# Two of the three split products of a tile put side by side: PEER queries, late up-projection tiles, second FFN

## The chip, the cores and the metric

The kernel runs on one core of one Trainium2 chip. The metric is device time in microseconds (us) of one launch; the kernel before takes 3022.41 us (median of three runs, 3020.68 to 3022.94). The core has TensorE (PE: products; PEld its weight loads), VectorE (DVE), ScalarE (ACT), GpSimd (POOL) and SyncE (SP, which issues most DMAs). Each works through its own instructions in the order in which the program lists them.

## The reference, cut to what matters

Two blocks of two layers work on 256 tokens of width 1024. The first block has a mixer and PEER in each of its layers, the second attention and a gated feed-forward network (FFN) in each. What the change touches:

```python
q = (xt @ wq).reshape(t, PEER_HEADS, D_KEY)        # 16 tiles of 128 query rows
s1 = einsum("thd,hnd->thn", q1, k1); s2 = ...      # scores against 128 + 128 keys
v1, i1 = lax.top_k(s1, TOPK); v2, i2 = ...         # then top 16 of the 16*16 sums
gates = softmax(sv)                                # of 16 of 16384 experts a head
hid = gelu(einsum("td,tkd->tk", xi, u_tab[ei]))    # up-projection
out = einsum("tk,tkd->td", gi * hid, v_tab[ei])    # down-projection
# FFN of the second block:  (silu(x @ Wg) * (x @ Wu)) @ Wo
```

## The kernel before, in words

Activations lie transposed, features on the 128 partitions and tokens (T = 256) along the free axis. Every large fp32 product is made of three: the weights `w` and the input `x` are each split in a high and a low part of type fp32r (wh, wl; hi, lo), and hi·wh, lo·wh and hi·wl are added up in PSUM. `gemm` (L464 to L475) issues these three for each of the kc slices of 128 input features, through `mm` (all at L430); a tile of 1024 input features has kc = 8, so 24 products of 128x256.

Weights come in tiles of 512 KB through `Stream`: SP loads each into one of four `st` buffers; two tiles before it is used, ACT rounds it (CAST `wh`, L381) and DVE subtracts (TENSOR_TENSOR `wl`, L381). There are three `wh`/`wl` buffers, so this split waits until PE is done with the tile three before.

PEER (its layers at about 143 to 960 us and 1104 to 1920 us) first makes the queries: 16 tiles from "wq". After tile b's products, `score(b)` (L1082 to L1094) has ACT copy the PSUM tile to `qt` (L1085) and PE multiply it by the keys into `sc0` and `sc1`; after every fourth tile ACT copies the scores out. On PE, score(b) stands behind the products of tile b+1; the tag `mm` has two PSUM buffers. While this runs, a generator `topk` (L1212 to L1349) puts the search for the best 16 (MAX, MAX_INDEX, MATCH_REPLACE on DVE) between the other work: after each weight tile, `pump` takes pieces from it up to a budget of estimated ns (PUMP0 500, later PUMP 1100 and PUMP2 1400). Then follow 128 "u" tiles (up-projection; PE also makes the gates by one-hot products, `gtok` tokens of them complete) and 128 "v" tiles (down-projection). The reference's picking of 16 experts is done densely: all 16384 hidden values are made and multiplied by gates that are mostly zero. `hid` (L1200 to L1210) finishes a u tile: ACT makes gelu from PSUM, DVE multiplies by the gates where they are complete.

`ffn` (L1845 to L1922) is called with N = 512 columns (first FFN, even layer, 2200 to 2580 us) and with N = 256 (second FFN, odd layer, 2819 to 3013 us). For each of NFF = 22 feature tiles it makes two products (tags mm0, mm1, two buffers each), silu on ACT and a product on DVE, which is split again into fh and fl; then 8 output tiles (out of tag mm0) end in `finish` (L1809, one DVE instruction for each token half).

The order on each engine is set when the program is built: the Python code gives it in outline, and a scheduler with its own estimates of time moves what is free to move.

Of the kernel before, what the change touches and what calls it, by code (L numbers as in the profile page):

```python
# [10 lines left out]
F32R = mybir.dt.float32r  # L11
# [401 lines left out]
class Builder:  # L413
# [50 lines left out]
    def gemm(self, ps, w, kc, rhs, k0=0, first=True, last=True, order=None):  # L464
        hi, lo = w
        order = order or range(kc)
        for n, k in enumerate(order):
            a = hi[:, k * P:(k + 1) * P]
            b = lo[:, k * P:(k + 1) * P]
            rh, rl = rhs(k0 + k)  # L470
            with self.after(self.gends[:1] if n == 0 and len(self.gends) in GP else []):
                self.mm(ps, a, rh, start=first and n == 0)
            self.mm(ps, a, rl)
            self.mm(ps, b, rh, stop=last and n == kc - 1)
        self.gends.append(self.lastmm)  # L475

    def rsq(self, ss, n, pool, tag="rs", bufs=None, ln=False, eps=EPS):
# [569 lines left out]
    def peer(self, l):  # L1047
        nc, tc = self.nc, self.tc
        with tc.tile_pool(name=f"pe{l}", bufs=1) as sp, tc.tile_pool(name=f"pew{l}", bufs=2) as wk, \
# [4 lines left out]
            self.iota8 = self.t(sp, [P, 16, 8], F16, tag="iota8")  # L1054
            self.iota4 = self.t(sp, [P, 4 * P], F16, tag="iota4")
            with tc.tile_pool(name=f"peh{l}", bufs=1) as hp:
                hi = self.t(hp, [P, KD, T], F32R, tag="hi")
                lo = self.t(hp, [P, KD, T], F32R, tag="lo")
                flat = big.rearrange("p j t -> p (j t)")
                front = Carve(flat[:, :4096], 4096)  # L1060
                tail = Carve(flat[:, J0 * T:], (P - J0) * T)
                pk = self.t(tail, [P, 2, 1024], tag="pk", bufs=1)
                for n in range(2):
                    nc.gpsimd.dma_start(pk[:, n], self.I["pk"][l, n])
                self.warm(pp, "g", WP[0], 2)
                ss = self.sumsq((self.t(self.psp, [P, 512], tag="pss", bufs=1) if FD & 1 else self.t(pp, [P, 512], tag="mm"))[:, :T])
                self.warm(pp, "g", WP[1], 2)
                r = self.rsq(ss, T, front, tag="nrm", bufs=1)
                self.norm(self.x, lambda k: self.g(f"norm2_g{l}", k), None, hi, lo, front, r)
                with self.after(self.nins):  # L1070
                    nc.vector.tensor_copy(self.iota8, self.iota[:, :16].unsqueeze(2).to_broadcast([P, 16, 8]))
                    nc.vector.tensor_copy(self.iota4.rearrange("p (i t) -> p i t", t=4),
                                          self.iota.unsqueeze(2).to_broadcast([P, P, 4]))
                nc.gpsimd.dma_start(self.xd[l], self.x)
                self.ohp = Carve(self.x.rearrange("p k t -> p (k t)"), KD * T)
                self.ocp = Carve(self.sreg, 4 * T)
                rhs = lambda k: (hi[:, k, :], lo[:, k, :])
                sc = [self.t(tail, [P, 16, P], tag="sc") for _ in range(2)]
                scp = None
                pend = []  # L1080

                def score(b, ps):  # L1082
                    nonlocal scp
                    qt = self.t(front, [P, T], tag="qt")
                    nc.scalar.copy(qt, ps)  # L1085
                    if b % 4 == 0:
                        scp = [self.t(pp, [P, 4, P], tag=f"sc{t}", bufs=1) for t in range(2)]
                    key = pk[:, b % 2, (b // 2) * P:(b // 2 + 1) * P]
                    for t in range(2):
                        self.mm(scp[t][:, b % 4, :], qt[:, t * P:(t + 1) * P], key, start=True, stop=True)  # L1090
                    if b % 4 == 3:
                        for t in range(2):
                            nc.scalar.copy(sc[t][:, b - 3:b + 1, :], scp[t])
                        self.scored = b + 1  # L1094

                self.J, self.gtok, self.scored = 0, 0, 0
                self.tkdone = False
                self.bg.append(self.topk(l, sc, tail, wk, pp))
                for b in range(16):
                    w = self.stream.get("wq", (l, b), 0, 1024)  # L1100
                    ps = self.t(pp, [P, 512], tag="mm")[:, :T]
                    self.gemm(ps, w, KD, rhs)
                    self.pump(PUMP0)
                    if pend:
                        score(*pend.pop())
                    pend.append((b, ps))
                score(*pend.pop())
                for j in range(P):
                    if j == J0:
                        while not self.tkdone:  # L1110
                            self.pump(1)
                    w = self.stream.get("u", (l, j), 0, 1024)
                    ps = self.t(pp, [P, 512], tag="mm")[:, :T]
                    self.gemm(ps, w, KD, rhs)
                    self.pump(PUMP if j < J0 else PUMP2)
                    if pend:
                        self.hid(*pend.pop(), wk)
                    pend.append((j, ps))
                self.hid(*pend.pop(), wk)
                self.drain()  # L1120
            if self.stop == f"hid{l}":
# [75 lines left out]
        if self.stop == f"peer{l}":  # L1197
            nc.sync.dma_start(self.dump["x"], self.x)

    def hid(self, j, ps, wk):  # L1200
        nc = self.nc
        tk = self.gtok
        dst = self.big[:, j, :]
        if tk:
            tmp = self.t(wk, [P, T], tag="gl")
            self.af(tmp[:, :tk], ps[:, :tk], AF.Gelu_apprx_tanh)
            nc.vector.tensor_mul(dst[:, :tk], dst[:, :tk], tmp[:, :tk])
        if tk < T:
            self.af(dst[:, tk:], ps[:, tk:], AF.Gelu_apprx_tanh)
        self.J = j + 1  # L1210

    def topk(self, l, sc, tl, wk, pp):  # L1212
# [632 lines left out]
    def ffn(self, l, N):  # L1845
        nc, tc = self.nc, self.tc
        with tc.tile_pool(name=f"ff{l}", bufs=1) as sp, tc.tile_pool(name=f"ffw{l}", bufs=2) as wk, \
                tc.tile_pool(name=f"ffp{l}", bufs=2, space=PSUM) as pp:
            fh = self.t(sp, [P, NFF, N], F32R, tag="fh")
            fl = self.t(sp, [P, NFF, N], F32R, tag="fl")  # L1850
            mb = self.t(wk, [P, KD * T], tag="mb", bufs=1)
            nw = Carve(mb, KD * T)
            md = iter(())
# [5 lines left out]
                    next(md, None)  # L1859

            with tc.tile_pool(name=f"ffh{l}", bufs=1) as hp:
                hi = self.t(hp, [P, KD, N], F32R, tag="hi")
                lo = self.t(hp, [P, KD, N], F32R, tag="lo")
                for m in range(N // T - 1, -1, -1):
                    W = (WF0, WF1)[l]
                    if m == 0:
# [7 lines left out]
                    self.modnorm(l, 1, m, hi[:, :, q], lo[:, :, q], nw, r)  # L1874
                rhs = lambda k: (hi[:, k, :], lo[:, k, :])
                for f in range(NFF):
                    pg = [self.t(pp, [P, 512], tag=f"mm{n}")[:, :N] for n in range(2)]
                    sl = self.t(wk, [P, N], tag="sl")
                    if f == 0 and N > T:
                        W = [self.stream.get("fi", (l, f, n), 0, 1024) for n in range(2)]  # L1880
                        for h in range(2):
                            q = slice(h * T, h * T + T)
                            for n in range(2):
                                hrhs = lambda k: (hi[:, k, q], lo[:, k, q])
                                self.gemm(pg[n][:, q], W[n], KD, hrhs, first=h == 0)
                        self.af(sl, pg[0], AF.Silu)
                    else:
                        for n in range(2):
                            w = self.stream.get("fi", (l, f, n), 0, 1024)
                            self.gemm(pg[n], w, KD, rhs)  # L1890
                            side()
                            if n == 0:
                                self.af(sl, pg[0], AF.Silu)
                    nc.vector.tensor_mul(sl, sl, pg[1])
                    nc.scalar.copy(fh[:, f, :], sl)
                    nc.vector.tensor_sub(fl[:, f, :], sl, fh[:, f, :])
# [3 lines left out]
            for b in range(KD):  # L1900
# [1 line left out]
                    self.tables(ARS)  # L1902
                split = b == KD - 1 and N > T
                W = []
                ps = self.t(pp, [P, 512], tag="mm0")[:, :N]
                k0 = 0
                for kc in kcs:
                    W.append(self.stream.get("fo", (l, b), k0 * P, kc * P))
                    if not split:
                        self.gemm(ps, W[-1], kc, lambda k: (fh[:, k, :], fl[:, k, :]), k0=k0, first=k0 == 0,  # L1910
                                  last=k0 + kc == NFF)
                    k0 += kc
                for m in range(N // T - 1, -1, -1):
                    q = slice(N - T - m * T, N - m * T)
                    if split:
                        ps = self.t(pp, [P, 512], tag=f"mm{m}")[:, :N]
                        k0 = 0
                        for w, kc in zip(W, kcs):
                            self.gemm(ps[:, q], w, kc, lambda k: (fh[:, k, q], fl[:, k, q]), k0=k0, first=k0 == 0,
                                      last=k0 + kc == NFF)  # L1920
                            k0 += kc
                    self.finish(l, 1, b, ps[:, q], m, wk)  # L1922

    def odd(self):
# [174 lines left out]
```

## Time and profile before

| | |
|---|---|
| Median of three runs | 3022.41 us |
| Profiled execution | 3020.7 us, its span 3018.9 us |
| PE busy | 2933.6 us (97%), 19072 products |
| PE's mean granted clock | 0.991 of full speed |
| DVE busy | 2250.0 us (75%) |
| ACT busy | 1704.3 us (56%) |
| Down-projection "v" tiles, both layers | about 2 x 360 us, not touched by the change |

Busy shares are averages over the whole span. Stages differ: in the u tiles PE is full and DVE half full, in the query stage both are full. Read a change from the stage in which it stands.

### The profile page before, as it was taken

The numbers are of one execution on the slowest core, as the hardware profiler recorded it, in microseconds if no ns is written. First come the engines' busy times: TensorE is split into PE (matmuls) and PEld (weight loads), VectorE is DVE, ScalarE is ACT, GpSimd is POOL, SyncE is SP. The second block draws the span as 40 slices with busy tenths as digits, with TensorE's granted clock in tenths as the row PEclk, the third lists the DMA queues.
The fourth block names the chain that finished last, engine by engine and source line by source line (L and its number), as shares of the span: only waits on it lengthen the run. The fifth ranks groups of instructions, "written<-read, shape, count | busy, mean of one in ns | idle before, by whom it ended". The sixth has DMA issues, their size and how long they took to land.

```text
span 3018.9 us, 50427 instructions
## 1 busy us (share of the span) xinstructions
PE 2933.6 (97%) x19072; PEld 2595.6 (86%) x19072; DVE 2250.0 (75%) x4353; ACT 1704.3 (56%) x2931; POOL 215.4 (7%) x259
## 2 busy tenths in 40 slices
PE   8999999999999899999999999998999999999999
PEld 7899999977888889999997788875688878976899
DVE  8799699699556969879969855677577773478654
ACT  7546799544444655589944444467532222377443
POOL 4200000000001710000000000100120001100100
PEclk8999999999999999999999999999999999999999
DMA  5456555588665445655568766511146553331454
GB/s 158 146 161 182 170 159 156 173 291 258 192 194 171 142 136 173 182 163 158 156 213 282 236 192 194 155 59 42 53 130 186 181 185 107 105 105 56 151 183 149
DMA packets 133603, 489.35 MB, mean 162 GB/s; under 512 B 15024, under 2 KB 15280, under 8 KB 132208
## 3 DMA queue, kind: packets, MB, share of 16 engines
q1 hardware_dynamic: 130608, 472.65, 51.0%
q0 software_dynamic: 2608, 13.44, 1.3%
q8 instruction: 150, 2.46, 0.3%
q14 instruction: 93, 0.76, 0.1%
q10 hardware_dynamic: 144, 0.05, 0.0%
HBM read 480.83 MB, written 5.24 MB: 161 GB/s over the span
## 4 chain that ended last, share of the span: by engine, by line
PE 57%; DVE 3%; ACT 2%; issue 1%; DMA 0%; DVEq 0%; ACTq 0%; SPq 0%
PE mm L430 39%; PE g L430 7%; PE sc L430 6%; PE s L430 3%; PE o L430 1%; PE pt L1752 1%; PE pss L430 1%; ACT wh L381 0%; DVE lo L637 0%; PE ss L430 0%; PE pss L1365 0%; ACT grsy L498 0%; DVE wl L381 0%; DVE hi L637 0%; DVE mb L637 0%
## 5 line engine op out<-in xcount | busy, mean ns | idle before, releaser
L381 ACT CAST wh<-st 128x1024 fp32r<-128x1024 f32 (+1 forms) x797 | 831.6, 1045 | 921.5 <-PE mm L430 506.7
L381 DVE TENSOR_TENSOR wl<-st,wh 128x1024 fp32r<-128x1024 f32 (+1 forms) x797 | 977.1, 1227 | 447.8 <-ACT wh L381 440.2
L430 PE MATMUL mm<-hi,wh 128*128 128x256 f32 (+1 forms) x3552 | 1083.0, 306 | 11.8 <-DVE hi L637 7.2
L430 PE MATMUL mm<-hi,wl 128*128 128x256 f32 (+1 forms) x3552 | 1066.0, 301 | 8.0 <-DVE wl L381 7.8
L430 PE MATMUL mm<-lo,wh 128*128 128x256 f32 (+1 forms) x3552 | 1065.3, 300 | 3.0 <-DVE lo L637 2.9
L430 PEld LDWEIGHTS mm<-hi,wh 128*128 128x128 f32 x3552 | 680.4, 192 | 44.6 <-issue 7.6
L430 PEld LDWEIGHTS mm<-hi,wl 128*128 128x128 f32 x3552 | 682.5, 192 | 30.2 <-DVE wl L381 9.2
L430 PEld LDWEIGHTS mm<-lo,wh 128*128 128x128 f32 x3552 | 683.3, 192 | 26.8 <-DVE lo L637 5.9
L430 PE MATMUL sc<-wl,wwh 128*128 128x512 f32 x496 | 195.1, 393 | 0.0
L430 PE MATMUL g<-wl,wwh 128*128 128x512 f32 x496 | 193.1, 389 | 0.0
L430 PE MATMUL g<-wh,wwl 128*128 128x512 f32 x496 | 193.1, 389 | 0.0
L430 PE MATMUL sc<-wh,wwl 128*128 128x512 f32 x496 | 193.1, 389 | 0.0
L430 PE MATMUL sc<-wh,wwh 128*128 128x512 f32 x496 | 192.3, 389 | 0.0
L430 PE MATMUL g<-wh,wwh 128*128 128x512 f32 x496 | 192.3, 389 | 0.0
L1154 ACT CAST wwh<-big 128x512 fp32r<-128x512 f32 x124 | 77.1, 624 | 148.4 <-PE g L430 148.3
L1329 ACT COPY sreg<-x 128x512 f16<-128x512 f16 x256 | 158.3, 661 | 0.0
L1397 DVE SCALAR_TENSOR_TENSOR sreg<-mb,silc,sreg 128x512 f32<-128x512 f32 x168 | 116.9, 745 | 10.8 <-DMA mb<-in_mod 10.5
L1397 DVE SCALAR_TENSOR_TENSOR sreg<-tl,silc,sreg 128x512 f32<-128x512 f32 x168 | 119.8, 747 | 4.7 <-DMA tl<-in_mod 4.6
L430 PE MATMUL mm<-fl,wh 128*128 128x256 f32 (+1 forms) x374 | 122.4, 327 | 0.0
L430 PE MATMUL mm<-fh,wh 128*128 128x256 f32 (+1 forms) x374 | 122.4, 327 | 0.0
L430 PE MATMUL mm<-fh,wl 128*128 128x256 f32 (+1 forms) x374 | 122.3, 327 | 0.0
L1155 DVE TENSOR_TENSOR wwl<-big,wwh 128x512 fp32r<-128x512 f32 x124 | 85.4, 690 | 48.1 <-ACT wwh L1154 48.0
(550 smaller groups left out, 4518.2 us busy)
## 6 DMA issues: line engine op xcount, KB each, us to landing
st<-in_u SPq DMA_DIRECT2D x256, 512.0 KB, 3.7
st<-in_v SPq DMA_DIRECT2D x256, 512.0 KB, 3.7
st<-in_fi SPq DMA_DIRECT2D x88, 512.0 KB, 3.4
st<-in_w SPq DMA_DIRECT2D x58, 512.0 KB, 3.7
tl<-in_mod SPq DMA_DIRECT2D x48, 512.0 KB, 4.9
mb<-in_mod SPq DMA_DIRECT2D x48, 512.0 KB, 4.3
st<-in_wq SPq DMA_DIRECT2D x32, 512.0 KB, 4.3
st<-in_fo SPq DMA_DIRECT2D x32, 512.0 KB, 3.6
```

The lines of the kernel that those rows point to most:

```text
L381: self.last = [b.nc.scalar.copy(hi, t).ins, b.nc.vector.tensor_sub(lo, t, hi).ins]
L430: self.lastmm = self.nc.tensor.matmul(out, lhsT=a, rhs=b, start=start, stop=stop, skip_group_check=True).ins
L1154: nc.scalar.copy(wh, big[:, j:j + 2, :])
L1155: nc.vector.tensor_sub(wl, big[:, j:j + 2, :], wh)
L1329: nc.scalar.copy(oc[m], o[:, m].rearrange("p i t -> p t i"))
L1397: nc.vector.scalar_tensor_tensor(a, w[:, k % 2], s, a, op0=OP.mult, op1=OP.add)
L1752: nc.tensor.transpose(pt[:, b, :], A[qt][:, b * P:(b + 1) * P], self.ident)
```

## The change

A function `gemm2` makes the three products as two instructions. High and low part of the input lie side by side in one buffer `hl` of [128, kc, 2, 256]; per slice, one product of 512 columns gives wh·hi in the left half of a PSUM bank and wh·lo in the right half, and one of 256 columns adds wl·hi to the left half. The columns streamed are the same, 768 for each slice; one product and one weight load fewer are issued. The two halves have to be added afterwards. The change uses `gemm2` in three places:

- the 16 query tiles of both PEER layers (2 x 16 x 8 = 256 slices); in `score` ACT copies the right half and DVE adds the left
- the u tiles whose gates are complete when they are made: 19 in each layer (2 x 19 x 8 = 304 slices); in `hid` ACT copies, DVE adds, ACT then makes gelu from SBUF, DVE multiplies
- the second FFN: 44 input tiles (352 slices) with copy and add, and 8 output tiles of 22 slices (176), where `finish` runs once for each half

Together 1088 slices. No DMA is added or taken away.

```diff
+    def gemm2(self, ps, w, kc, hl, k0=0, first=True, last=True):
+        hi, lo = w
+        for n in range(kc):
+            self.mm(ps, hi[:, n * P:(n + 1) * P], hl[:, k0 + n], start=first and n == 0)
+            self.mm(ps[:, :T], lo[:, n * P:(n + 1) * P], hl[:, k0 + n, 0], stop=last and n == kc - 1)
+        self.gends.append(self.lastmm)
...
                 def score(b, ps):
                     qt = self.t(front, [P, T], tag="qt")
-                    nc.scalar.copy(qt, ps)
+                    nc.scalar.copy(qt, ps[:, T:])
+                    nc.vector.tensor_add(qt, qt, ps[:, :T])
...
-                    self.gemm(ps, w, KD, rhs)
+                    self.gemm2(ps, w, KD, hl)
                     self.pump(PUMP0)
...
+                    pair = self.gtok == T
+                    if pair:
+                        self.gemm2(ps, w, KD, hl)
+                    else:
+                        self.gemm(ps[:, :T], w, KD, rhs)
...
+        if pair:
+            tmp = self.t(wk, [P, T], tag="gl")
+            nc.scalar.copy(tmp, ps[:, T:])
+            nc.vector.tensor_add(tmp, tmp, ps[:, :T])
+            self.af(tmp, tmp, AF.Gelu_apprx_tanh)
+            nc.vector.tensor_mul(dst, dst, tmp)
...
+                                self.gemm2(pg[n], w, KD, hl)
+                                sm = self.t(wk, [P, T], tag=f"sm{n}")
+                                nc.scalar.copy(sm, pg[n][:, T:])
+                                nc.vector.tensor_add(sm, sm, pg[n][:, :T])
+                                pg[n] = sm
...
+                    if N == T:
+                        self.finish(l, 1, b, ps[:, T:], m, wk)
                     self.finish(l, 1, b, ps[:, q], m, wk)
```

DVE, query stage of the first PEER layer, before, from the split of tile 7 (`wl36`) on. `big` is the buffer in which the top-k search works, `mm` a PSUM tile:

```order
L381 TENSOR_TENSOR wl36_1892<-st36_1755,wh36_1891 128x1024
L1228 MAX big_185_1656<-big_185_1656 128x8 x8
L1229 MAX_INDEX big_185_1656<-big_185_1656 128x8
L1231 MATCH_REPLACE big_185_1656<-big_185_1656 128x128
L1229 MAX_INDEX big_185_1656<-big_185_1656 128x8 x4
L1231 MATCH_REPLACE big_185_1656<-big_185_1656 128x128
L1229 MAX_INDEX big_185_1656<-big_185_1656 128x8 x3
L381 TENSOR_TENSOR wl37_1933<-st37_1791,wh37_1932 128x1024
L1232 MAX big_185_1656<-big_185_1656 128x8 x2
L381 TENSOR_TENSOR wl38_1972<-st38_1825,wh38_1971 128x1024
```

The same place now; `mm_220` and `mm_222` are the query tiles 4 and 5:

```order
L381 TENSOR_TENSOR wl36_1855<-st36_1746,wh36_1854 128x1024
L1093 TENSOR_TENSOR big_185_1656<-big_185_1656,mm_220_1831 128x256
L1246 MAX big_185_1656<-big_185_1656 128x8 x8
L1247 MAX_INDEX big_185_1656<-big_185_1656 128x8
L1249 MATCH_REPLACE big_185_1656<-big_185_1656 128x128
L1247 MAX_INDEX big_185_1656<-big_185_1656 128x8 x4
L1249 MATCH_REPLACE big_185_1656<-big_185_1656 128x128
L1247 MAX_INDEX big_185_1656<-big_185_1656 128x8
L381 TENSOR_TENSOR wl37_1889<-st37_1775,wh37_1888 128x1024
L1247 MAX_INDEX big_185_1656<-big_185_1656 128x8 x2
L1093 TENSOR_TENSOR big_185_1656<-big_185_1656,mm_222_1860 128x256
L1250 MAX big_185_1656<-big_185_1656 128x8 x2
```

The top-k pieces stand where they stood but for two of MAX_INDEX; an add of 128x256 now stands behind each `wl`, for tile 5 with a piece of the search between the two.

ACT in the u tiles with complete gates, before, from the rounding of the weights of u tile 118 on (`gl` is the gelu's result):

```order
L381 CAST wh163_7675<-st163_7543 128x1024
L498 ACTIVATE gl_829_7706<-mm_826_7647 128x256
L381 CAST wh164_7709<-st164_7577 128x1024
L498 ACTIVATE gl_831_7740<-mm_828_7681 128x256
L381 CAST wh165_7743<-st165_7611 128x1024
L498 ACTIVATE gl_833_7774<-mm_830_7715 128x256
```

And now:

```order
L381 CAST wh163_7518<-st163_7410 128x1024
L1218 COPY gl_828_7541<-mm_825_7496 128x256
L505 ACTIVATE gl_826_7513<-gl_826_7513 128x256
L505 ACTIVATE gl_828_7541<-gl_828_7541 128x256
L381 CAST wh164_7546<-st164_7438 128x1024
L1218 COPY gl_830_7569<-mm_827_7524 128x256
L381 CAST wh165_7574<-st165_7466 128x1024
L1218 COPY gl_832_7597<-mm_829_7552 128x256
L505 ACTIVATE gl_830_7569<-gl_830_7569 128x256
```

Before, each rounding of weights is followed by one gelu. Now a copy takes the gelu's place, and the gelus come in twos, so that every second rounding stands behind two of them. On DVE the multiplications come in twos in the same way, between the adds.

## Rows read from the trace of the kernel before

**Rows 1.** The page: busy us (share of the span), instructions.

```profile
PE 2933.6 (97%) x19072; PEld 2595.6 (86%) x19072; DVE 2250.0 (75%) x4353; ACT 1704.3 (56%) x2931; POOL 215.4 (7%) x259
```

**Rows 2.** The page: chain of work that ended last, shares by engine.

```profile
PE 57%; DVE 3%; ACT 2%; issue 1%; DMA 0%; DVEq 0%; ACTq 0%; SPq 0%
```

**Rows 3.** Windows: us; busy (instructions) of PE, PEld, DVE, ACT, POOL; PEclk, DMA share, GB/s.

```profile
160.00:200.00 40.00, 40.00 (x339) 40.00 (x339) 37.91 (x180) 18.75 (x30) 0.00 (x0) 1.00 0.53 151
200.00:240.00 40.00, 40.00 (x334) 39.84 (x333) 40.00 (x192) 23.11 (x33) 0.00 (x0) 1.00 0.59 181
240.00:280.00 40.00, 39.89 (x333) 39.69 (x332) 39.09 (x117) 22.63 (x35) 0.00 (x0) 1.00 0.60 175
560.00:600.00 40.00, 40.00 (x332) 39.82 (x331) 21.52 (x29) 18.44 (x28) 0.00 (x0) 1.00 0.61 184
2840.00:2880.00 40.00, 40.00 (x335) 40.00 (x335) 22.29 (x28) 18.80 (x28) 0.00 (x0) 1.00 0.56 185
1960.00:2160.00 200.00, 190.06 (x757) 131.75 (x756) 144.84 (x358) 137.42 (x309) 3.11 (x6) 1.00 0.14 43
```

**Rows 4.** Timeline of PE, second FFN: start us, duration us, instruction.

```profile
2896.94 0.28 PE L430 MATMUL mm<-lo,wh 128*128 128x256 f32 x1
...
2899.82 0.28 PE L430 MATMUL mm<-lo,wh 128*128 128x256 f32 x1
```

**Rows 5.** Timeline of PE, products of 512 columns.

```profile
859.83 0.39 PE L430 MATMUL g<-wh,wwh 128*128 128x512 f32 x1
...
861.87 0.39 PE L430 MATMUL sc<-wh,wwl 128*128 128x512 f32 x1
```

**Rows 6.** Timeline of PE, query stage: first score, and two later ones.

```profile
151.55 0.71 PE L430 MATMUL sc<-big 128*128 128x128 f32 x4 [1.05 <-ACT big L1085]
...
158.29 0.61 PE L430 MATMUL sc<-big 128*128 128x128 f32 x4
...
161.61 0.61 PE L430 MATMUL sc<-big 128*128 128x128 f32 x4
```

**Rows 7.** Timeline of DVE, query stage: weight splits and first row of three groups.

```profile
151.26 2.44 DVE L381 TENSOR_TENSOR wl<-st,wh 128x1024 fp32r<-128x1024 f32 x2 [1.96 <-ACT wh L381]
...
163.91 1.64 DVE L1228 MAX8 big<-big 128x8 f32<-128x128 f32 x8
...
177.81 1.63 DVE L1228 MAX8 big<-big 128x8 f32<-128x128 f32 x8
...
181.45 1.21 DVE L381 TENSOR_TENSOR wl<-st,wh 128x1024 fp32r<-128x1024 f32 x1
...
182.57 0.09 DVE L1229 MATCH_VALUE_LOAD big<-big 128x8 f32 x1
...
191.44 1.24 DVE L1228 MAX8 big<-big 128x8 f32<-128x128 f32 x6
```

**Rows 8.** Lines L854 (DVE add) and L1085 (ACT copy): durations ns min/median/max.

```profile
L854 DVE TENSOR_TENSOR x<-x,mm x8: 414/421/422, 121.1 to 1094.2; 128x256 f32<-128x256 f32 x8
...
L1085 ACT COPY big<-mm x32: 361/366/375, 151.1 to 1159.8; 128x256 f32<-128x256 f32 x32
```

**Rows 9.** Timeline of ACT and DVE, a late u tile.

```profile
555.67 1.05 ACT L381 CAST wh<-st 128x1024 fp32r<-128x1024 f32 x1 [1.55 <-PE mm L430]
...
556.62 0.38 ACT L498 ACTIVATE gl<-mm 128x256 f32<-128x256 f32 x1
...
556.75 1.22 DVE L381 TENSOR_TENSOR wl<-st,wh 128x1024 fp32r<-128x1024 f32 x1 [1.32 <-ACT wh L381]
...
557.89 0.42 DVE L1207 TENSOR_TENSOR big<-big,gl 128x256 f32<-128x256 f32 x1
```

**Rows 10.** Timeline of DVE and SP: the end.

```profile
3013.37 0.48 DVE L1809 SCALAR_TENSOR_TENSOR x<-mm,mt,x 128x256 f32<-128x256 f32 x1 [6.28 <-PE mm L430]
...
3013.88 0.35 SPq L2071 DMA_DIRECT2D out<-x  x1
```

More of the change, by code (lines that the diff above doesn't have):

```diff
@@ L1056, in peer @@
             with tc.tile_pool(name=f"peh{l}", bufs=1) as hp:
-                hi = self.t(hp, [P, KD, T], F32R, tag="hi")
-                lo = self.t(hp, [P, KD, T], F32R, tag="lo")
+                hl = self.t(hp, [P, KD, 2, T], F32R, tag="hl")
+                hi, lo = hl[:, :, 0], hl[:, :, 1]
                 flat = big.rearrange("p j t -> p (j t)")
@@ L1100, in peer @@
                     w = self.stream.get("wq", (l, b), 0, 1024)
-                    ps = self.t(pp, [P, 512], tag="mm")[:, :T]
-                    self.gemm(ps, w, KD, rhs)
+                    ps = self.t(pp, [P, 512], tag="mm")
+                    self.gemm2(ps, w, KD, hl)
                     self.pump(PUMP0)
@@ L1112, in peer @@
                     w = self.stream.get("u", (l, j), 0, 1024)
-                    ps = self.t(pp, [P, 512], tag="mm")[:, :T]
-                    self.gemm(ps, w, KD, rhs)
+                    ps = self.t(pp, [P, 512], tag="mm")
+                    pair = self.gtok == T
[3 more added lines that the diff above has]
+                        self.gemm(ps[:, :T], w, KD, rhs)
                     self.pump(PUMP if j < J0 else PUMP2)
@@ L1117, in peer @@
                         self.hid(*pend.pop(), wk)
-                    pend.append((j, ps))
+                    pend.append((j, ps, pair))
                 self.hid(*pend.pop(), wk)
@@ L1198, in peer, with hid @@
             nc.sync.dma_start(self.dump["x"], self.x)
-    def hid(self, j, ps, wk):
+    def hid(self, j, ps, pair, wk):
         nc = self.nc
@@ L1203, in hid @@
         dst = self.big[:, j, :]
-        if tk:
+        if pair:
[4 more added lines that the diff above has]
+            nc.vector.tensor_mul(dst, dst, tmp)
+        elif tk:
             tmp = self.t(wk, [P, T], tag="gl")
@@ L1208, in hid @@
         if tk < T:
-            self.af(dst[:, tk:], ps[:, tk:], AF.Gelu_apprx_tanh)
+            self.af(dst[:, tk:], ps[:, tk:T], AF.Gelu_apprx_tanh)
         self.J = j + 1
@@ L1848, in ffn @@
                 tc.tile_pool(name=f"ffp{l}", bufs=2, space=PSUM) as pp:
-            fh = self.t(sp, [P, NFF, N], F32R, tag="fh")
-            fl = self.t(sp, [P, NFF, N], F32R, tag="fl")
+            if N > T:
+                fh = self.t(sp, [P, NFF, N], F32R, tag="fh")
+                fl = self.t(sp, [P, NFF, N], F32R, tag="fl")
+            else:
+                fhl = self.t(sp, [P, NFF, 2, T], F32R, tag="fhl")
+                fh, fl = fhl[:, :, 0], fhl[:, :, 1]
             mb = self.t(wk, [P, KD * T], tag="mb", bufs=1)
@@ L1861, in ffn @@
             with tc.tile_pool(name=f"ffh{l}", bufs=1) as hp:
-                hi = self.t(hp, [P, KD, N], F32R, tag="hi")
-                lo = self.t(hp, [P, KD, N], F32R, tag="lo")
+                if N > T:
+                    hi = self.t(hp, [P, KD, N], F32R, tag="hi")
+                    lo = self.t(hp, [P, KD, N], F32R, tag="lo")
+                else:
+                    hl = self.t(hp, [P, KD, 2, T], F32R, tag="hl")
+                    hi, lo = hl[:, :, 0], hl[:, :, 1]
                 for m in range(N // T - 1, -1, -1):
@@ L1876, in ffn @@
                 for f in range(NFF):
-                    pg = [self.t(pp, [P, 512], tag=f"mm{n}")[:, :N] for n in range(2)]
+                    pg = [self.t(pp, [P, 512], tag=f"mm{n}") for n in range(2)]
                     sl = self.t(wk, [P, N], tag="sl")
@@ L1889, in ffn @@
                             w = self.stream.get("fi", (l, f, n), 0, 1024)
-                            self.gemm(pg[n], w, KD, rhs)
+                            if N > T:
+                                self.gemm(pg[n], w, KD, rhs)
+                            else:
+                                self.gemm2(pg[n], w, KD, hl)
[3 more added lines that the diff above has]
+                                pg[n] = sm
                             side()
@@ L1904, in ffn @@
                 W = []
-                ps = self.t(pp, [P, 512], tag="mm0")[:, :N]
+                ps = self.t(pp, [P, 512], tag="mm0")
                 k0 = 0
@@ L1908, in ffn @@
                     W.append(self.stream.get("fo", (l, b), k0 * P, kc * P))
-                    if not split:
+                    if N == T:
+                        self.gemm2(ps, W[-1], kc, fhl, k0=k0, first=k0 == 0, last=k0 + kc == NFF)
+                    elif not split:
                         self.gemm(ps, W[-1], kc, lambda k: (fh[:, k, :], fl[:, k, :]), k0=k0, first=k0 == 0,
@@ L1921, in ffn @@
                             k0 += kc
+                    if N == T:
+                        self.finish(l, 1, b, ps[:, T:], m, wk)
                     self.finish(l, 1, b, ps[:, q], m, wk)
```

## The prediction

> **What bounds the kernel now.** I read the page first: PE is busy for 97% of the span [rows 1], and the chain of work that ended last runs over PE for 57% of the span and over every other engine for 3% or less [rows 2]. So a PE instruction less is time less, wherever PE has no other reason to wait. Then the windows, stage by stage [rows 3]. In the late u tiles (560 to 600 us) and in the second FFN (2840 to 2880) PE is busy for 40.00 of 40 us, DVE for 21.52 and 22.29, ACT for under 19: room for work on DVE. In the query stage and just behind it (160 to 280) it is otherwise: PE 40.00, 40.00 and 39.89, and DVE 37.91, 40.00 and 39.09. There two engines are full at once, and what is put on DVE there has no gap to go into. Most of the first window's 2.09 us of DVE idle is no reserve either: the top-k search begins only at 163.91 [rows 7]. The change takes time from PE in three stages and gives DVE work in the same three, one of them this one.
>
> **What one pair saves.** Products of 256 columns in the second FFN start 24 apart in 2.88 us, 120.0 ns each [rows 4]; products of 512 columns start nine apart in 2.04 us, 226.7 ns each [rows 5]. Twice the columns cost 106.7 ns more, so 13.3 ns belong to the instruction. Three products of 256 take 360.0 ns, one of 512 and one of 256 take 346.7: 13.3 ns saved a slice, 0.107 us a tile of eight slices, 14.5 us over 1088 slices if nothing else happens. The 24 products of a tile go from 2.88 to 2.77 us.
>
> The Trainium skill, "TensorE: Matmul & The Clock Gate", section "Back-to-back issue gap", gives an isolated gap of columns by 2.4 GHz plus about 2.5 ns. For these fp32r products the trace disagrees, 120.0 and 226.7 ns where that rule has 109 and 216. By the rule a slice would save 2.5 ns, all slices 2.7 us; since the fixed part is measured here, the sum goes by the rows.
>
> **Second FFN: -6.6.** 528 slices by 13.3 ns are -7.0 us. The 44 copies (0.37 us on ACT) and 44 adds (0.42 us on DVE) [rows 8] come to 14 of each in 40 us: 5.2 us on ACT beside 18.80, 5.9 on DVE beside 22.29 [rows 3]. Tags mm0 and mm1 have two buffers each, so the copy and add of a tile have until three tiles later, over 8 us; this work lies beside PE. If that cover were gone, each tile would wait about 0.8 us (copy and add in series), 35 us in all; with half of both engines free I see no reason for it. At the end it does show: the last output tile has two `finish` instructions where there was one of 0.48 us, between PE's last product and the output DMA [rows 10]; since one starts before the other's recorded end, +0.4.
>
> **Late u tiles: -2.4.** 304 slices save 4.0 us if nothing waits. In the trace ACT rounds the next weights at 555.67, makes gelu at 556.62, DVE splits at 556.75 (behind the rounding) and multiplies at 557.89 [rows 9]; the last product of the tile in question starts at 555.47, 0.20 us before that rounding. PE could use the PSUM buffer again when the gelu was done, at 557.00. Now the buffer is free when the add is done, which on DVE stands behind the split, where the multiplication stood: 557.89 + 0.42 = 558.31, 2.84 us after that product's start. PE wants the buffer 0.12 + 2.77 = 2.89 us after it. That is a tie. But ACT's order now has two gelus in a row before every second rounding, and the second of them waits for the add: about 558.3 + 0.38, 558.7 with its signal, where the next rounding could start at about 558.55. So every second tile can be late by up to 0.2 us, which would eat both tiles' 0.21. Bounds: -4.0 (no wait) and +1.7 (a wait of 0.15 in each of the 38 tiles, 5.7 - 4.0). I take a wait behind every fourth tile or so, -1.2 a layer.
>
> **Query stage: +14.0.** PE's tile takes 3.32 us here (161.61 - 158.29 [rows 6]: 2.88 of products, 0.44 of score), four tiles 13.28. DVE's period for four tiles, search and splits, is (191.44 - 163.91)/2 = 13.77 us [rows 7]. So DVE was already 0.49 us a group slower than PE, which the splits' lead of two tiles absorbed. Now four adds join each period. One lasts 0.42 us [rows 8], but DVE's instructions start before the one ahead has ended in the record (a split of 1.21 us has its follower 1.12 after its start [rows 7]), so 0.33 to 0.42; I take 0.38. DVE's period becomes 13.77 + 1.52 = 15.29, PE's own work 13.28 - 0.43 = 12.85. And the lead no longer helps: score(b) waits for add(b) itself, and that stands on DVE behind the split of tile b+3 and, as the order shows, for tile 5 behind a piece of search as well (177.81 to 181.45 is such a piece, 3.6 us [rows 7]). PE's next tile but one waits for the same add through the two `mm` buffers. What queues behind it on DVE is the next split, so PE's wait comes back to DVE as nothing gained. PE takes DVE's pace: 15.29 - 13.28 = 2.0 us a group, three groups between tile 4 and the end of the queries, +6.0 a layer; the saving of PE's pairs in them is gone.
>
> Ahead of the groups the first score waits too. It starts at 151.55, released by ACT's copy [rows 6]; DVE's split of tile 3 starts at 151.26 [rows 7], and its add can follow only at 152.38, ending at 152.80: +1.3. Three tiles between save 0.3. Together +7.0 a layer, +14.0 for both. Following the order instruction by instruction with these durations gives the same within half a microsecond, with waits of about 2 us at scores 5, 9 and 13. PE does not win it back: behind the queries it is full again [rows 3], and everything of the search is late by the same amount. Bounds: -1.5 a layer (every add hidden, the pairs' saving of 14 tiles kept, the first two tiles being bound by their inputs) and +8.6 (1.3, adds of 0.42, and half a microsecond more for each of the three long pieces of search).
>
> **Even attention stage: 0.** The diff does not touch it, but the scheduler now lists ACT's and DVE's instructions there in another order. PE idles 9.94 us of the 200 between 1960 and 2160 [rows 3]. What a new order does to that can't be read from here: bounds -5 and +5, half of that idle time gone or added; I take 0, the present order being as good a guess as any.
>
> **Sum.** 14.0 - 2.4 - 6.6 = +5.0. The profiled execution took 3020.7 us, so 3025.7; the median of the runs shown is 1.7 above that execution, so 3027.4.
>
> **The rivals.**
> *The adds are hidden.* The search gives way, scores don't wait, and PE keeps all its savings: 2 x -1.5, -4.0, -6.6 = -13.6, 3008.8. For it: DVE is busy for only 75% [rows 1], and ACT, which could hold up the copy, has half its time free. Against it: 40.00 of 40 on DVE just where the adds go, and fixed places in its order. 15%.
> *Half is won back.* Score's waits are shorter than the period says, because DVE's idle time of about 3 us in 160 to 280 and the lead of the splits behind the queries take up part of them: +3.5 a layer in place of +7.0, so -2.0, 3020.4. 25%.
> *A wait in the even stage.* The new order there adds 5 us to PE's idle 9.94: +10.0, 3032.4. It decides as soon as some operand of the attention comes later than before; nothing in the trace speaks for or against. 15%.
> *No gain from pairing.* Products of 512 and 256 columns in turn, each with its own weights, are not in this trace; if the pair takes 360 ns as before, the FFN gives +0.4 and the u tiles nothing, +14.4, 3036.8. Against it: both lengths have the same 13.3 ns. This is also about where the page's rule would end. 5%.
>
> **How the numbers follow.** My forecast has 40%: 3027.4, by itself 3023 to 3032. The range of 8 in 10 reaches down towards the hidden adds and up to the unpaired case: 3012 to 3036. About 0.2%, 6 us, is what can be told from no change. Faster than 3016.4 is the first rival and a little of the second, 19%; slower than 3028.4 is about two fifths of the forecast, the even stage, the unpaired case and the rest, 39%; between, 42%.
>
> **What would show it.** In the changed profile: PE idle before `sc` of 1 to 2.5 us, released by DVE's add in `score`, four or more times a layer; the first u tile about 7 us later in the first layer and 13 in the second; PE busy below 37 of 40 in 160 to 200. Pairs starting 347 ns apart, tiles of 2.77 us in the second FFN, and that FFN 6 to 7 us shorter. In the late u tiles waits of PE of under 0.25 us. I am wrong if PE stays at 40.00 in 160 to 200, if the pair takes 360 ns, or if the stages between 1950 and 2820 us change their length by more than 3 us.

## The result: 3043.0 us, slower by 0.7%

| | before | after |
|---|---|---|
| Median | 3022.47 us | 3043.02 us |
| Ratio, 95% interval | | 1.0068 (1.0055 to 1.0081) |
| Profiled execution, its span | 3020.7, 3018.9 us | 3042.9, 3040.8 us |
| PE products | 19072 | 17984 |

The sign was forecast, the size was not: +5 us forecast, +20.5 us measured, outside the range. 19072 - 17984 = 1088 products are gone, as the change says, and the chain of work that ended last now runs over PE for 87% and over DVE for 8% of the span. In the changed profile's page (busy times of the engines, then the shares of the chain) [rows 1, 2]:

```profile
PE 2931.3 (96%) x17984; PEld 2537.9 (83%) x17984; DVE 2292.1 (75%) x4475; ACT 1728.6 (57%) x3013; POOL 215.9 (7%) x259
...
PE 87%; DVE 8%; ACT 3%; issue 1%; DMA 0%; DVEq 0%; ACTq 0%; SPq 0%
```

PE's busy time is only 2.3 us less although over a thousand products are gone, in part because the granted clock was at its lower level for 70.1 us of the span instead of 59.0; and its idle time went from 85.3 us to 109.5.

**Where the time went.** Both programs split the same 797 weight tiles in the same order on DVE, so the start of a split is a landmark that both traces have (they are counted from 0). How much later each starts after the change (us), from DVE's rows at L381:

| landmark | later by |
|---|---|
| weight tile 30, start of the first query stage | -0.03 |
| 154, first paired u tile of layer 0 | +10.72 |
| 300, near the end of layer 0's "v" tiles | +15.02 |
| 330, second query stage | +14.99 |
| 450, before the paired u tiles of layer 1 | +24.27 |
| 600, near the end of layer 1's "v" tiles | +26.95 |
| 640, first FFN | +26.84 |
| 734, second FFN, first tiles | +28.27 |
| last product | +21.39 |
| output DMA | +21.91 |

So the two query stages cost 10.7 and 9.3 us, the late u tiles 4.3 and 2.7, the stages between (the attention of the second block and the first FFN) 1.3 together; the second FFN gained 6.9, and its end gave back 0.5.

**The query stages.** First two of the windows of [rows 3], then PE's waits for scores, in the timeline of PE of the changed kernel:

```profile
160.00:200.00 40.00, 36.21 (x211) 31.29 (x211) 35.42 (x157) 16.33 (x27) 0.00 (x0) 0.96 0.43 134
200.00:240.00 40.00, 38.34 (x304) 37.15 (x303) 39.15 (x192) 19.31 (x29) 0.00 (x0) 1.00 0.51 158
```

```profile
152.84 0.71 PE L430 MATMUL sc<-big 128*128 128x128 f32 x4 [2.26 <-DVE big L1093]
...
172.66 0.71 PE L430 MATMUL sc<-big 128*128 128x128 f32 x4 [1.78 <-DVE big L1093]
...
189.22 0.71 PE L430 MATMUL sc<-big 128*128 128x128 f32 x4 [1.62 <-DVE big L1093]
...
204.57 0.71 PE L430 MATMUL sc<-big 128*128 128x128 f32 x4 [1.54 <-DVE big L1093]
```

Scores 0, 5, 9 and 13 wait, each released by DVE's add at L1093. From the start of the last product to the score these places lost 2.42, 1.94, 1.78 and 1.70 us against a product's normal spacing, scores 7, 11 and 15 another 0.9 together; of the first, 1.21 was there before [rows 6]. That is 7.5 us a layer. Then the clock: windows of 5 us behind the first two of these waits, and one around the third.

```profile
155.00:160.00 5.00, 5.00 (x27) 4.39 (x26) 1.06 (x1) 1.32 (x2) 0.00 (x0) 0.80 0.44 140
...
175.00:180.00 5.00, 5.00 (x26) 4.36 (x25) 3.84 (x20) 1.32 (x2) 0.00 (x0) 0.75 0.36 105
...
185.00:190.00 5.00, 3.38 (x22) 2.77 (x21) 5.00 (x26) 1.97 (x4) 0.00 (x0) 1.00 0.36 102
```

The granted clock stands behind POOL's count: 0.80 and 0.75 over five microseconds in which PE was busy throughout (1.00 around the third wait). In each of the two some five pairs took 641 ns each, 427 and 214, where a pair otherwise takes 347: PE ran at its lower level, 1.2 instead of 2.4 GHz. Each such stretch costs about 1.5 us; there are two in the first layer and one in the second, which is just the difference between 10.7 and 9.3. Waits 7.5, clock 3.0, pairs -1.5 make 9.0 of the 10.7; the last 1.7 (the same in both layers) lies in gaps of 0.1 us or less around the scores and was not followed further.

**The late u tiles.** DVE's timeline at the first paired tiles of layer 0, then PE's at the same place:

```profile
564.66 1.22 DVE L381 TENSOR_TENSOR wl<-st,wh 128x1024 fp32r<-128x1024 f32 x1
565.79 0.75 DVE L1219 TENSOR_TENSOR gl<-gl,mm 128x256 f32<-128x256 f32 x2
566.69 0.76 DVE L1221 TENSOR_TENSOR big<-big,gl 128x256 f32<-128x256 f32 x2
571.94 1.23 DVE L381 TENSOR_TENSOR wl<-st,wh 128x1024 fp32r<-128x1024 f32 x1 [4.49 <-ACT wh L381]
```

```profile
563.13 0.28 PE L430 MATMUL mm<-hl,wl 128*128 128x256 f32 x1
566.35 0.54 PE L430 MATMUL mm<-hl,wh 128*128 128x512 f32 x1 [2.94 <-DVE gl L1219]
```

Two adds in a row (x2): those of the first and of the second paired tile. Both stand on DVE behind a split which can't begin before PE is through with the second of them, at 563.13. So PE has no free PSUM buffer for the third tile, and stands for 2.94 us until the add; the prediction's sign for this stage was waits of under 0.25 us. It stands there in both layers (3.10 us lost each time), and in layer 0 a stretch at a clock of 0.53 follows (566.4 to 570). In the tiles behind, small waits of 0.04 to 0.11 us, up to 0.23 together behind every second tile, come to 1.0 to 1.1 us in 41 us, against 1.55 that the pairs save there.

**The second FFN** does what was worked out. Ten pairs in PE's timeline, and the end on DVE and SP [rows 4, 10]:

```profile
2899.62 0.39 PE L430 MATMUL mm<-hl,wh 128*128 128x512 f32 x1
2899.85 0.28 PE L430 MATMUL mm<-hl,wl 128*128 128x256 f32 x1
...
2903.08 0.39 PE L430 MATMUL mm<-hl,wh 128*128 128x512 f32 x1
```

```profile
3034.76 1.00 DVE L1827 SCALAR_TENSOR_TENSOR x<-mm,mt,x 128x256 f32<-128x256 f32 x2 [5.80 <-PE mm L430]
...
3035.79 0.35 SPq L2108 DMA_DIRECT2D out<-x  x1
```

3.46 us for ten pairs is 346 ns, so the fixed cost of 13.3 ns an instruction holds. The Trainium skill, "TensorE: Matmul & The Clock Gate", section "Back-to-back issue gap", would have this pair at about 325 ns (512 and 256 columns by 2.4 GHz, 2.5 ns each, an estimate from that page's formula for an isolated product); for these products the trace disagrees.

### The profile page after: what moved, and what is told of

Read it like the earlier page. It is cut to its first block, busy times and chain, and to the rows that moved or that the text cites. A ratio compares the mean times of both kernels' runs of the same rounds, so it can differ in the third digit from the quotient of the medians.

```text
span 3040.8 us, 48474 instructions
## 1 busy us (share of the span) xinstructions
PE 2931.3 (96%) x17984; PEld 2537.9 (83%) x17984; DVE 2292.1 (75%) x4475; ACT 1728.6 (57%) x3013; POOL 215.9 (7%) x259
## 4 chain that ended last, share of the span: by engine, by line
PE 87%; DVE 8%; ACT 3%; issue 1%; DMA 0%; DVEq 0%; ACTq 0%; SPq 0%
PE mm L430 54%; PE g L430 13%; PE sc L430 12%; PE s L430 4%; DVE wl L381 2%; PE o L430 1%; DVE cacc L903 1%; PE pss L430 1%; PE pt L1770 1%; ACT wh L381 1%; PE pss L1383 1%; PE ss L430 0%; ACT grsy L505 0%; DVE lo L644 0%; DVE hi L644 0%
## 5 line engine op out<-in xcount | busy, mean ns | idle before, releaser
L381 ACT CAST wh<-st 128x1024 fp32r<-128x1024 f32 (+1 forms) x797 | 831.8, 1045 | 892.4 <-PE mm L430 427.2
L381 DVE TENSOR_TENSOR wl<-st,wh 128x1024 fp32r<-128x1024 f32 (+1 forms) x797 | 980.1, 1231 | 434.6 <-ACT wh L381 429.1
L430 PE MATMUL mm<-hl,wh 128*128 128x256 f32 (+1 forms) x4400 | 978.4, 311 | 14.5 <-DVE gl L1219 5.9
L430 PEld LDWEIGHTS mm<-hl,wh 128*128 128x128 f32 x4400 | 716.9, 192 | 58.8 <-issue 8.1
L430 PE MATMUL mm<-hl,wl 128*128 128x256 f32 x2656 | 751.7, 283 | 0.5 <-DVE wl L381 0.5
L430 PEld LDWEIGHTS mm<-hl,wl 128*128 128x128 f32 x2656 | 510.2, 192 | 1.1 <-DVE wl L381 0.8
L430 PE MATMUL mm<-hi,wh 128*128 128x512 f32 (+1 forms) x896 | 318.2, 358 | 9.0 <-DVE hi L644 5.9
L430 PE MATMUL mm<-hi,wl 128*128 128x512 f32 (+1 forms) x896 | 313.7, 351 | 6.1 <-DVE wl L381 6.1
L430 PE MATMUL mm<-lo,wh 128*128 128x512 f32 (+1 forms) x896 | 312.3, 350 | 1.6 <-DVE lo L644 1.5
L430 PEld LDWEIGHTS mm<-hi,wh 128*128 128x128 f32 x896 | 171.3, 193 | 40.6 <-issue 6.1
L430 PEld LDWEIGHTS mm<-hi,wl 128*128 128x128 f32 x896 | 172.2, 192 | 29.2 <-DVE wl L381 7.6
L430 PEld LDWEIGHTS mm<-lo,wh 128*128 128x128 f32 x896 | 172.1, 192 | 24.1 <-DVE lo L644 3.6
```

Of the source, the lines that this page charges most:

```text
L381: self.last = [b.nc.scalar.copy(hi, t).ins, b.nc.vector.tensor_sub(lo, t, hi).ins]
L430: self.lastmm = self.nc.tensor.matmul(out, lhsT=a, rhs=b, start=start, stop=stop, skip_group_check=True).ins
```

## The experiments

All medians are beside runs of the kernel before on the same chip (3022.5 to 3023.1 us). Ratios are to it, with the 95% interval. "Later by" is the shift of splits as in the table above; where a stage is spoken of, it is from the trace, since the attention stages of the second block differ by up to 5 us each between these profiles, in order and in clock, with no edit in them. Small shifts are not to be read either: in the kernel with the FFN alone, which leaves PEER as it was, the second query stage starts 1.7 us later and ends 0.7 later.

**One stage at a time.** Where a stage is not paired, its products go back to

```diff
-                    self.gemm2(ps, w, KD, hl)
+                    self.gemm(ps[:, :T], w, KD, rhs)
```

and its copy and add go with it. The FFN alone:

> The second FFN alone is paired; queries and u tiles are as before. Theory (the loss comes from DVE's adds in the query stage and the late u tiles, each stage by itself): the FFN keeps its gain, -5 to -6 us, so 3017; the splits of weight tiles 0 to 720 come within 1 us of their times before. Rival (the loss comes from the scheduler's new order of the stages that were not edited, or from pairs as such): not faster than 3022.

Measured 3016.61 us, 0.9978 (0.9968 to 0.9987), faster by 5.9. The two PEER layers end 0.1 and 0.5 us later than before. As the theory had it for the time; only the stages between the PEER layers and the second FFN, 7.1 us longer in this profile (0.5 to 7.6 later), missed the "within 1 us".

The query tiles alone:

> The query tiles alone are paired. Theory: the waits of PE for the adds, +7.6 us a layer, less 1.5 for the pairs, and one or two stretches at the lower granted clock of 1.5 us each behind them: +9 to +11 a layer, 3042. Rival (the loss needs the late u tiles as well, since it is the late search that meets them): +7 a layer or less, 3036 or less.

Measured 3042.43 us, 1.0063 (1.0046 to 1.0080). Later by 11.2 us behind the first query stage and 20.0 behind the second, with the same waits:

```profile
153.32 1.23 PE L430 MATMUL sc<-big 128*128 128x128 f32 x4 [2.25 <-DVE big L1093]
173.13 0.71 PE L430 MATMUL sc<-big 128*128 128x128 f32 x4 [1.78 <-DVE big L1093]
189.69 0.71 PE L430 MATMUL sc<-big 128*128 128x128 f32 x4 [1.56 <-DVE big L1093]
```

The loss of the query stage is its own; it needs no other stage.

The late u tiles alone:

> The late u tiles alone are paired. Theory: one wait of about 3 us a layer at the third paired tile, where both adds stand behind a split that can't start before the second paired tile is done, sometimes 1.5 for the lower clock behind it, and no gain later since ACT's gelus in twos eat it: +2.5 to +4.5 a layer, 3029. Rival (the wait was made by the late search of the paired queries): -1 to -2 a layer, 3020.

Measured 3032.49 us, 1.0033 (1.0020 to 1.0046). Later by 4.3 us behind layer 0 and 6.8 behind layer 1, so 4.3 and 2.5 a layer; another 4.5 us of this profile's difference lie in the stages up to the second FFN. PE's wait is there though the search is on time (in this and some later kernels the add stands at L1218):

```profile
555.59 0.47 PE L430 MATMUL mm<-hl,wh 128*128 128x512 f32 x1 [2.94 <-DVE gl L1218]
```

**Without the add.** In the query stage, paired:

```diff
-                    nc.scalar.copy(qt, ps[:, T:])
-                    nc.vector.tensor_add(qt, qt, ps[:, :T])
+                    nc.scalar.copy(qt, ps[:, :T])
```

> The query tiles alone are paired, and the add is left out: ACT copies the left half, so the part lo*wh is missing from the queries. Theory (the add on DVE is the whole loss): -1.5 us a layer and no wait above half a microsecond but the first score's, 3019.5. Rival (pairs of 512 and 256 columns, or the fuller PSUM tile, cost something there by themselves): 3025 or more.

Measured 3023.58 us, 1.0001 (0.9991 to 1.0011), which is no difference. In the trace the query stages are without loss: earlier by 0.3 us behind the first and 1.2 behind the second, though they began 0.7 and 0.8 later; no wait but the first score's, and PE full where it was at 36.21:

```profile
160.00:200.00 40.00, 40.00 (x253) 35.90 (x252) 37.88 (x178) 19.11 (x32) 0.00 (x0) 1.00 0.51 154
```

So the add on DVE is the whole loss there, not the pair. Counted from their own starts the two stages took 1.0 and 2.0 us less, together the 3 expected, as far as such shifts can be read; what the stages between took back and 4 us in the attention stages covered it in that profile.

**A third PSUM buffer for the u tiles.** In PEER, with the FFN paired and the queries not:

```diff
-                    ps = self.t(pp, [P, 512], tag="mm")
+                    ps = self.t(pp, [P, 512], tag="mm", bufs=3)
```

> Second FFN and late u tiles paired, queries as before, and three PSUM buffers instead of two for the tag mm in PEER. Theory (in the u tiles PE waits for a free PSUM buffer, which the add on DVE releases a tile late): the 3 us wait at the third paired tile and the loss of the steady tiles go, each layer gains up to 2 us; with the FFN's -5.9 the time is 3013. Rival (PE is held there by something else, the splits behind two gelus for one): u tiles stay at +2.5 to +4.3 a layer, 3023.

Measured 3012.95 us, 0.9961 (0.9948 to 0.9974), 10 us faster than before. The long wait has become a short one, before the fourth paired tile instead of the third, and layer 0 gains 1.6 us from its first paired tile on and layer 1 1.8, of 2.0 possible. First PE, then DVE at the same place:

```profile
554.40 0.47 PE L430 MATMUL mm<-hl,wh 128*128 128x512 f32 x1 [0.17 <-DVE gl L1218]
```

```profile
552.70 1.22 DVE L381 TENSOR_TENSOR wl<-st,wh 128x1024 fp32r<-128x1024 f32 x1
553.84 0.75 DVE L1218 TENSOR_TENSOR gl<-gl,mm 128x256 f32<-128x256 f32 x2
```

Both adds still stand behind one split, as in the change. So at this place it was the buffer and not another order that took the wait away.

**Scores two tiles behind.** Query tiles alone paired, adds on DVE, three buffers, and

```diff
-                    if pend:
-                        score(*pend.pop())
+                    if len(pend) > 1:
+                        score(*pend.pop(0))
```

> Query tiles alone paired, adds on DVE as in the change, but score(b) stands two tiles behind instead of one, with three PSUM buffers. Theory (DVE's work per four tiles, 15.3 us, exceeds PE's and sets the pace): most of the loss stays, +4 to +7 us a layer without the first score's wait, 3033. Rival (only the place of the add matters, one tile more of slack hides it): -1 us a layer, 3020.

Measured 3020.18 us, 0.9988 (0.9979 to 0.9998). My theory fell: no wait of note but the first score's, 1.1 us earlier behind the first query stage. With the adds on DVE, PE is full:

```profile
160.00:200.00 40.00, 40.00 (x256) 35.99 (x255) 36.67 (x158) 19.06 (x30) 0.00 (x0) 1.00 0.51 157
```

DVE's work of four tiles is not 15.3 us here. Between the first rows of two groups of the search lie 13.1 and 13.2 us (180.75, 193.82, 207.06), with four splits and three or four adds among them, but less of the search: 6 MATCH_REPLACE instead of 8, 13 MAX instead of 16. The rest of the search stands in the u tiles.

**The add on GpSimd.** FFN and queries paired, ACT copies both halves:

```diff
-                    nc.scalar.copy(qt, ps[:, T:])
-                    nc.vector.tensor_add(qt, qt, ps[:, :T])
+                    qh = self.t(front, [P, 2 * T], tag="qh")
+                    nc.scalar.copy(qh, ps)
+                    nc.gpsimd.tensor_add(qt, qh[:, :T], qh[:, T:])
```

> Second FFN and query tiles paired, u tiles as before; in score ACT copies both halves (512 columns) to SBUF and GpSimd adds them there, nothing is added on DVE. Theory (DVE is the full engine, ACT and GpSimd have room): the query stage gains its 1.5 us a layer or is within 1 us of before, 3014 with the FFN's -5.9. Rival (any second step between products and score costs, or GpSimd slows DVE down): +3 us a layer or more, 3022 or more.

Measured 3015.45 us, 0.9978 (0.9968 to 0.9988). The query stage is within 1 us of before (later by 0.6 behind the first, by 0.0 behind the second; counted from their starts, 0.5 and 1.3 shorter), as the theory's second case has it; the pairs' 1.5 us a layer don't show in full. GpSimd takes 0.73 to 1.81 us for an add that takes DVE 0.42 [rows 8]; two of the 32:

```profile
157.46 1.28 POOL L1094 TENSOR_TENSOR big<-big 128x256 f32<-128x256 f32 x1 [1.67 <-ACT big L1093]
161.09 1.30 POOL L1094 TENSOR_TENSOR big<-big 128x256 f32<-128x256 f32 x1 [2.35 <-ACT big L1093]
```

All three stages paired, this add and three buffers:

> All three stages paired, with the add of the query stage on GpSimd as in the kernel with GpSimd's add, and three PSUM buffers for mm. Theory: the gains add up, -5.9 for the FFN, -1 a layer for the queries, -1.5 a layer for the u tiles: 3011. Rival (the stages hinder each other): 3017 or more, not better than the FFN alone.

Measured 3013.80 us, 0.9967 (0.9953 to 0.9981): better than before, but no better than without paired queries.

**What the third buffer does.** Query tiles alone paired, score one tile behind as in the change, three buffers:

> Query tiles alone paired, adds on DVE, score(b) one tile behind as in the change, three PSUM buffers for mm. It parts the two things that the kernel with late scores changed together. Theory (score itself waits for the add, so the place of the score is what matters): waits before sc stay, +3 to +9 us a layer, 3030 or more. Rival (the missing thing was a PSUM buffer for the products behind): no waits but the first, -1 a layer, 3020.5.

Measured 3019.84 us, 0.9992 (0.9983 to 1.0002). My theory fell again, and the rival had the time right: no wait of note but the first score's (1.90 us), and 0.8 us earlier behind the first query stage.

```profile
160.00:200.00 40.00, 40.00 (x252) 35.72 (x252) 37.25 (x160) 19.07 (x30) 0.00 (x0) 1.00 0.49 155
...
280.00:320.00 40.00, 40.00 (x340) 39.90 (x339) 31.96 (x57) 27.25 (x42) 0.00 (x0) 1.00 0.58 179
```

The order of this kernel says more. With two buffers the products of tile b+2 need the buffer that copy and add of tile b read, so PE can't go past tile b+1 before add(b), wherever score(b) stands; in the change every score stands right behind tile b+1. With three the scheduler puts scores later, for instance score 3 behind 13 of the 16 products of tile 5, and spreads the search thinner: DVE is busy for 31.96 us in 280 to 320, where it was 27.62 before. The added work lies there, where DVE had room. So, as built, this kernel has its scores nearly two tiles behind like the one before it, and the two don't part the buffer from the place of the score.

The control, nothing paired and three buffers:

> Nothing paired, three PSUM buffers for mm in PEER: the control for the kernels with three buffers. Theory (before, nothing but the first score of a layer waits for a buffer): -0.5 to -1.5 us a layer at most, 3021 or within measurement of 3022.5. Rival (the third buffer, not the pairs, is what made those kernels faster): 3018 or less.

Measured 3022.84 us, 1.0002 (0.9993 to 1.0011). The buffer by itself gives nothing in the time and nothing in the late u tiles, where it counts only with the pairs. In the query stages of its trace it does give something with nothing paired, 2.0 and 1.9 us, which later stages take back; with the queries paired as well the stages are 1.3 and 2.2 us shorter. So beside the buffer the pairs of the query tiles no longer cost anything, but no run shows that they gain.

**Together.** All three stages paired, three buffers, scores two tiles behind:

> All three stages paired, three PSUM buffers for mm, score(b) two tiles behind, adds on DVE. Theory (with one tile more of slack every add is hidden): -5.9 for the FFN, -2 a layer for the u tiles, -1.3 a layer for the queries: 3010. Rival (the search pushed out of the query stage comes back as waits in the u tiles): 3014 or more.

Measured 3011.74 us, 0.9967 (0.9955 to 0.9979). And the same with the last output tile not paired:

> As the kernel with all three stages paired and late scores, but the last output tile of the second FFN is not paired (22 slices), so one finish stands at the end instead of two. Theory: the 22 slices lose 0.3 us, the end gains 0.4: no difference that can be measured, 3010; in the trace the last DVE instruction starts 0.4 us or less after the last product. Rival (the second finish costs more than it seems, 1 us or more): 3009.

Measured 3013.61 us, 0.9969 (0.9958 to 0.9981): the same within the interval. At its end one finish stands instead of two (0.90 us from the last product's start at 3006.73 to the DMA, where the changed kernel has 1.42):

```profile
3007.11 0.48 DVE L1828 SCALAR_TENSOR_TENSOR x<-mm,mt,x 128x256 f32<-128x256 f32 x1 [6.08 <-PE mm L430]
...
3007.63 0.35 SPq L2109 DMA_DIRECT2D out<-x  x1
```

The kernel with paired FFN and u tiles and a third buffer, and this one with everything, can't be told apart; both beat the kernel before by about 10 us and the change by about 30.

## Why the prediction was wrong, point by point

Of the changed profile's +21.9 us the sum had +5.0. The late u tiles account for 9.4 of the 16.9 missing, the query stages for 6.0, the stages between for 1.3, the second FFN for 0.2.

*What one pair saves, and the second FFN* were right: 13.3 ns a slice, 346 ns a pair, -6.9 and +0.5 at the end where -7.0 and +0.4 stood. The experiment with the FFN alone gave -5.9.

*The query stage, "+14.0"*, has the right place and the right waits: scores 0, 5, 9 and 13, about 2 us each, were named, and 7.5 us of added waits a layer stand against 7.3 (1.3 and 6.0). The term is too small by 6, and most of this has a name: the lower clock behind some of the waits, 3.0 and 1.5 us, which the step did not count at all. The windows of before showed a clock of 1.00 in the first query stage [rows 3], and I took it as given in a stage that was about to get waits that it did not have.

The reason given for the waits, "PE takes DVE's pace: 15.29 - 13.28", holds for the order of the change: DVE's second group takes 15.35 us, and so does PE from score 9 to score 13 (189.22 to 204.57). But it is no bound, since the search is not work that must lie there. With a third buffer, the same adds on the same engine cost nothing that the time shows, and part of the search stands in tiles where DVE is idle. In the change PE can't go past tile b+1 before add(b), and the search stands ahead of that add in a fixed order. What a third buffer, a later score and a thinner search do apart from each other was not separated: the scheduler changes the other two when given the first. The upper bound was also added up wrongly, 8.6 where its terms make 9.0; the layers lost 10.7 and 9.3.

*The late u tiles, "-2.4"*, is the step that failed outright, +7.0 measured and +1.7 the worst bound. It was worked out from the repeating tiles; there the "tie" and the 0.2 us behind every second tile are what the trace shows, and they take about two thirds of the gain, not the two fifths that I chose. But the first tiles of the stage stand in another order than the repeating ones, both adds behind one split, and that order was there to be read. It costs 3.1 us a layer and once 1.5 for the clock.

*The even attention stage, "0"*, is -0.1 in the changed profile (tiles 600 to 640). The other 1.4 up to the second FFN, most of it in the odd attention stage, had no term. In the experiments' profiles these stages moved by up to 5 us each with no edit in them, so that the bounds of 5 were of the right size and the 0 partly luck.

*The rivals.* "The adds are hidden" (3008.8) is what three buffers come near to, 3011.7 to 3013.8, though with the search moved and no gain shown for the queries. "No gain from pairing" is refuted by the 346 ns.

## What to carry to other kernels

A step added between a product and the release of its PSUM buffer was hidden here where PE had another buffer to go on with (the second FFN, and PEER with three, but for the first score of a layer), and cost waits of up to 3.1 us where it had none: count buffers before instructions. Read the first and the last tiles of a stage in the new order, not only the repeating ones. Where an in-order engine is full of filler such as a search, ask whether the filler can move before taking its pace for a bound; and where a full TensorE gets waits of some 2 us, leave room for the lower clock behind them.

## What the runs showed of the hardware that I had not expected

Waits of the same length are not always followed by the lower clock. In the change, behind the first score's wait of 2.4 us products ran at half speed (427 ns for 512 columns) for some 3 us in both layers; behind score 5's 1.94 us they did in the first layer and not in the second; behind 1.78 and 1.70 us they did not, and behind the 3.1 us in the u tiles they did in the first layer and not in the second. In the kernel with the query tiles alone, second layer, it was the other way round: none behind the first score's wait of 2.4 us, but a stretch behind score 5's 1.94 us. Its windows behind these two:

```profile
1125.00:1130.00 5.00, 5.00 (x33) 4.45 (x32) 1.88 (x3) 1.32 (x2) 0.00 (x0) 1.00 0.66 210
1143.20:1146.60 3.40, 3.40 (x13) 2.92 (x13) 3.40 (x18) 0.00 (x0) 0.00 (x0) 0.50 0.78 248
```

So the cost of a wait of 2 to 3 us here was its length or its length and about 1.5 us more.
